# Inverse levels and tokens of a state-space layer done per whole block, at places beside the chain's stages of the same array tile

## The chip, the cores and the metric

The kernel runs on one core of one Trainium2 chip. The metric is the device time of one execution in microseconds (us), median of 3 runs.

## What is computed

A backbone of two layers over 512 latent and 256 context tokens of width 1024. In each layer a combined projection feeds two mixers side by side, a depthwise convolution of 31 taps with group norm, and a bidirectional RWKV-7 recurrence over 8 heads of 64; an output projection, and a SwiGLU feed-forward follow, all with modulation from the condition vectors. The recurrence is, per head and direction:

```python
def step(s, inp):
    r_t, k_t, v_t, w_t, kk_t, b_t = inp
    sa = -jnp.einsum("bhvk,bhk->bhv", s, kk_t)
    s = (s * w_t[:, :, None, :] + sa[..., None] * b_t[:, :, None, :]
         + v_t[..., None] * k_t[:, :, None, :])
    y = jnp.einsum("bhvk,bhk->bhv", s, r_t) if emit else None
    return s, y
```

It runs forward and backward over the context, and from the two final states over the latents. `y_f + y_b`, normalised per head, gated and joined with the convolution, goes through `w_out`.

## The kernel before

**Tiling.** The recurrence is done in chunks of 64 tokens. Two heads (a pair, 128 partitions) and both directions go together, so a layer has 4 pairs. The 12 chunks of a pair are 3 blocks of 4 chunks (`s` = 0 to 3), so a layer has 12 blocks `b` = 0 to 11. A block holds 8 (chunk, direction) places `q` for each of the two heads `hh`; a half `hf` is two of the four chunks.

**Steps of a block.** They are Python generators; each `yield` ends one step.
- `prep(b)`, 3 steps: decay, keys and so on into `KR` and `bk` (ScalarE, VectorE).
- `z_part(b)`, 3 steps: `grams` multiplies `bk` with `KR` on TensorE and masks the products on VectorE into `G`, one half a step; then `base(b)` inverts the 16x16 diagonal blocks of the chunk matrices. It writes `G` to DRAM (`d`), reads the diagonals back as `Dt`, runs 15 rounds of two VectorE operations on `xtmp` and `XT`, each dependent on the one before, copies `XT` once on ScalarE, and writes the result into an image in DRAM (`dimg`).
- `t_part(b, hf)`, 4 steps: `inverses` reads the image into `Tm` by DMA; `levels` grows the inverse from 16 to 64 with small products (`Tm`,`G` and `Tm`,`W` in tiles of 64x64, then 32x32) and copies between them; the last step puts `KR` into `G` for the chain.
- `tokens(b, hf)`, 2 steps: transposes of `bk` into `tT` and of the values into `UV`.
- `chain(b, s)`, 3 steps for each of four chunks: the serial part, from state `S` to the next: products `UV`,`G` (tile 128x64), copy to `Z`, `Z`,`Tm` (64x64), copy to `UV`, `UV`,`tT` (128x64), new `S`.

**Order.** TensorE's order is the program's order (`manual_schedule`); the other engines' orders are made by a scheduler from it. `weave` makes the program's order: each lane is `(first, slots, n, generator)`, its `n` steps stand at `first + slots*(i+1)/n` of a block of 16 slots, and all lanes of a block are sorted by that place. The lanes of block `b` hold the projection of later columns (`proj`), the modulation (`ada`), `chains(b)` at slots 1.33, 2.67, ... 16, convolution taps on VectorE, and the preparation of later blocks: `z_part(b + 2)`, `prep(b + 2)`, `t_part(b + 1, 0)`, and `t_part(b, 1)`. The places are in `PLAN`, one entry a layer; `prologue` holds those ahead of block 0, in units of a projection of 768 columns.

**Buffers.** `pd`, `pw`, `pc` are PSUM pools of 3, 3 and 2 banks; the levels and the tokens use `pw`, the chain `pc`. `Tm`, `tT` and `UV` have 4 buffers of half a block each. Every small operation is recorded under the line of a helper (`mm` 234, `act` 222, `tt` 228, `stt` 225), so that the trace is read by tile names.

Of the kernel before, what the change touches and what calls it, by code (L numbers as in the profile page):

```python
# [20 lines left out]
T = SX + SC  # L21
# [59 lines left out]
def _pack(i):  # L81
# [45 lines left out]
    for nf in FPARTS:  # L127
# [22 lines left out]
         lanes={"chains": (0, 16), "t1": (0, 4), "t0": (12, 4), "tok1": (0.6, 3.26), "tok0": (13, 2), "prep": (2, 4),  # L150
                "z": (9, 4), "bonus": (3.89, 12.11), "pair_prep": (8, 8), "pair_out": (0, 13)},
         prologue={"pair_prep": (-1.3, 1.2), "prep0": (-0.3, 0.8), "z0": (0.9, 0.58), "tok00": (1.99, 1.08), "tok01": (1.94, 0.38), "prep1": (2.4, 1.0),
                "z1": (3.58, 0.6), "t0": (3.89, 0.86), "tok10": (4.12, 0.2)},
# [4 lines left out]
         lanes={"chains": (0, 16), "t1": (0, 4), "t0": (12.5, 3.5), "tok1": (0, 2.35), "tok0": (13, 2), "prep": (2, 4),  # L158
                "z": (9, 5.03), "bonus": (1.41, 13.65), "pair_prep": (7.33, 7.84), "pair_out": (0, 13)},
         prologue={"pair_prep": (-1.7, 1.2), "prep0": (-0.44, 0.74), "z0": (0.93, 0.52), "tok00": (1.52, 0.47), "tok01": (1.79, 0.39), "prep1": (1.97, 0.98),  # L160
                "z1": (3.6, 0.6), "t0": (3.98, 0.73), "tok10": (4.3, 0.3)},
# [9 lines left out]
def net(ctx: ExitStack, tc: tile.TileContext, I, out):  # L171
# [369 lines left out]
    for l in range(DEPTH):  # L541
# [213 lines left out]
        def prep(b):  # L755
# [42 lines left out]
            BS[b] = dict(KR=KR, bk=bk, vr=vr, pc=pc, emit=emit, G={}, tT={}, UV={}, T={})  # L798
# [35 lines left out]
        def tokens(b, hf):  # L834

            p, gi = divmod(b, 3)
            P, B = PS[p], BS[b]
            bk = B["bk"]
            tT = s2.tile([128, 2, 4, 64], F32, tag="tT", name=nm("tT"), bufs=4)
            UV = s2.tile([128, 4, 2, 64], F32, tag="UV", name=nm("UV"), bufs=4)  # L840
            B["tT"][hf] = tT
            B["UV"][hf] = UV
            pt = [bank(), bank()]
            for s in range(2):
                for d in range(2):
                    cc = 2 * hf + s
                    o = 64 * (2 * s + d)
                    for hh in range(2):
                        hs = slice(64 * hh, 64 * hh + 64)
                        PE.transpose(pt[hh][:, o:o + 64],  # L850
                                     bk[hs, d, cc, hh:hh + 2, :].rearrange("p j t -> p (j t)"), ident[hs, hs])
            for hh in range(2):
                act(tT[:, hh, :, :], pt[hh][:, 0:256].rearrange("p (q j) -> p q j", j=64))
            yield
            pv = bank()
            for s in range(2):
                for d in range(2):
                    cc = 2 * hf + s
                    c0 = C * nat(0, gi, cc)
                    src = B["vr"][:, cc, :] if d else u[f"v{p}"][:, c0:c0 + 64]  # L860
                    o = 128 * (2 * s + d)
                    PE.transpose(pv[0:64, o:o + 128], src, ident)  # L862
            for hh in range(2):
                act(UV[64 * hh:64 * hh + 64, :, hh, :],
                    pv[0:64].rearrange("p (q h j) -> p q h j", q=4, h=2)[:, :, hh, :])
            yield
# [29 lines left out]
        def inverses(b, hf):  # L896

            Tm = s2.tile([128, 4, 2, 64], F32, tag="Tm", name=nm("Tm"), bufs=4)
            for hh in range(2):
                w = 64 - 64 * hh  # L900
                nc.sync.dma_start(out=Tm[w:w + 64].rearrange("p q x c -> p q (x c)"),
                                  in_=dimg[b % 3][8 * hf + 4 * hh:8 * hf + 4 * hh + 4, 0:8192]
                                  .rearrange("q (r c) -> r q c", c=128))
            BS[b]["T"][hf] = Tm

        def levels(b, hf):

            B = BS[b]
            Gt, Tm = B["G"][hf], B["T"][hf]
            lm = lmask.rearrange("p (x t) -> p x t", x=2)  # L910
            pW = bank()
            for q in range(4):
                for hh in range(2):
                    w = slice(64 - 64 * hh, 128 - 64 * hh)
                    mm(pW[w, 64 * q:64 * q + 64], Gt[w, hh, q, 0:64], Tm[w, q, 0, :])
            W = s2.tile([128, 4, 64], F32, tag="W", name=nm("W"))
            act(W.rearrange("p q t -> p (q t)"), pW[:, 0:256])
            yield
            pX = bank()
            for q in range(4):  # L920
                for hh in range(2):
                    w = slice(64 - 64 * hh, 128 - 64 * hh)
                    mm(pX[w, 64 * q:64 * q + 64], W[w, q, :], Tm[w, q, 1, :])
            for q in range(4):
                for hh in range(2):
                    w = slice(64 - 64 * hh, 96 - 64 * hh)
                    mm(pX[w, 256 + 32 * q:288 + 32 * q], Tm[w, q, 1, 0:32], W[w, q, 0:32])
            for hh in range(2):
                w = slice(64 - 64 * hh, 96 - 64 * hh)
                V.copy_predicated(out=Tm[w, :, 0, 0:32], mask=lm[w, 0:1, 0:32].to_broadcast([32, 4, 32]),  # L930
                                  data=pX[w, 256:384].rearrange("p (q t) -> p q t", t=32))
            V.copy_predicated(out=Tm[:, :, 1, :], mask=lm[:, 1:2, :].to_broadcast([128, 4, 64]),
                              data=pX[:, 0:256].rearrange("p (q t) -> p q t", t=64))
            yield
            pW = bank()
            W = s2.tile([128, 4, 64], F32, tag="W", name=nm("W"))
            for q in range(4):
                for hh in range(2):
                    w = 64 - 64 * hh
                    mm(pW[w + 32:w + 64, 32 * q:32 * q + 32], Gt[w:w + 32, hh, q, 32:64], Tm[w:w + 32, q, 0, 0:32])  # L940
            for hh in range(2):
                w = slice(96 - 64 * hh, 128 - 64 * hh)
                act(W[w, :, 0:32], pW[w, 0:128].rearrange("p (q t) -> p q t", t=32))
            yield
            pX = bank()
            for q in range(4):
                for hh in range(2):
                    w = 64 - 64 * hh
                    mm(pX[w:w + 32, 32 * q:32 * q + 32], W[w + 32:w + 64, q, 0:32], Tm[w + 32:w + 64, q, 1, 32:64])
            for hh in range(2):  # L950
                w = slice(64 - 64 * hh, 96 - 64 * hh)
                act(Tm[w, :, 1, 32:64], pX[w, 0:128].rearrange("p (q t) -> p q t", t=32))

            for hh in range(2):
                act(Gt[64 - 64 * hh:128 - 64 * hh, hh, :, 0:64].rearrange("p (s d) t -> p d s t", d=2),
                    B["KR"][64 * hh:64 * hh + 64, :, 2 * hf:2 * hf + 2, 0, :])
            yield

        def chain(b, s):
# [3 lines left out]
            Gt, tT, UV, Tm = (B[k][s // 2] for k in ("G", "tT", "UV", "T"))  # L963
# [8 lines left out]
            for d, hh in DH:  # L972
# [3 lines left out]
                mm(pz[w, 64 * d:64 * d + 64], Gt[k, hh, q, 0:64], UV[k, q, hh, :])  # L976
# [15 lines left out]
            for d, hh in DH:  # L992
                w = slice(64 - 64 * hh, 128 - 64 * hh)
                mm(pu[w, 64 * d:64 * d + 64], Tm[w, 2 * s_ + d, 1, :], Z[w, 64 * d:64 * d + 64])
            pu3 = pu[:, 0:128].rearrange("p (d t) -> p d t", d=2)
            with soon():
                act(UV[64:128, 2 * s_:2 * s_ + 2, 0, :], pu3[64:128], AF.Copy, scale=-1.0)
                ts(UV[0:64, 2 * s_:2 * s_ + 2, 1, :], pu3[0:64], -1.0, 0.0)
            yield

            if not fin:
                pm = bank("c")
                for d, hh in DH:
                    hs = slice(64 * hh, 64 * hh + 64)
                    mm(pm[hs, 64 * d:64 * d + 64], tT[:, hh, 2 * s_ + d, :], UV[:, 2 * s_ + d, hh, :])
                Sn = s2.tile([128, 2, 64], F32, tag="S", name=nm("S"))
                with soon():
# [8 lines left out]
                    Un = BS[bn]["UV"][sn // 2]  # L1016
                    act(Un[64:128, 2 * (sn % 2):2 * (sn % 2) + 2, 0, :], Sn[0:64])
                    act(Un[0:64, 2 * (sn % 2):2 * (sn % 2) + 2, 1, :], Sn[64:128])
                P["S"] = Sn
            if emit:  # L1020
                for d, hh in DH:
                    hs = slice(64 * hh, 64 * hh + 64)
                    q = 2 * s_ + d
                    mm(py[hs, 64 * d:64 * d + 64], UV[:, q, hh, :], Gt[:, hh, q, 64:128], S is None and d == 0, d == 1)
# [137 lines left out]
        def t_part(b, hf):  # L1162
            inverses(b, hf)
            yield from levels(b, hf)

        def chains(b):
            for s in range(4):
# [4 lines left out]
        with tc.manual_schedule(engines={mybir.EngineType.PE}):  # L1172
            for name, ps in zip(FIRST, pf):
# [3 lines left out]
            start = {"pair_prep": (pair_prep(0), 3), "prep0": (prep(0), 3), "z0": (z_part(0), 3), "tok00": (tokens(0, 0), 2),  # L1177
                     "tok01": (tokens(0, 1), 2), "prep1": (prep(1), 3), "z1": (z_part(1), 3), "t0": (t_part(0, 0), 4),
                     "tok10": (tokens(1, 0), 2)}
# [6 lines left out]
            for b in range(12):  # L1186
# [9 lines left out]
                lane("t1", t_part(b, 1), 4)  # L1196
# [197 lines left out]
```

## Time and profile before

| | |
|---|---|
| median of 3 runs | 2247.91 us (2246.09 to 2260.29) |
| the profiled execution's own time | 2251.84 us |
| its span | 2250.0 us |
| TensorE busy | 2134.0 us (95%) |
| VectorE, ScalarE, GpSimd busy | 1333.6, 952.3, 193.0 us |
| mean granted clock | 0.975 |
| mixing stage of layer 0, of layer 1 | about 105 to 590 us, about 1345 to 1815 us |

The span is the time from the program's first instruction to its last, the execution's time the whole on the device. The granted clock is the share of full speed that TensorE's clock got. A busy TensorE is not one at its peak, since its instructions overlap.

### The profile page before, as it was taken

What the parts mean: (1) busy time and instruction counts of PE and PEld (TensorE: products, weight loads), DVE (VectorE), ACT (ScalarE), POOL (GpSimd) and SP (SyncE); (2) the same over time, 40 slices, a digit from 0 to 9 for tenths busy, and PEclk for the clock granted to TensorE, in tenths of its full rate; (3) what the DMA queues carried; (4) which work ended last, traced back from release to release, by engine and by line L of the source; (5) the groups of instructions that cost most, each with busy time, mean ns of one, the idle gap of its engine ahead of it and who ended that gap; (6) DMA issues with size and microseconds to landing.
All of it is one profiled execution on the core that took longest, in us unless ns stands there. A gap on an engine that the chain in (4) does not pass through costs nothing.

```text
span 2250.0 us, 46614 instructions
## 1 busy us (share of the span) xinstructions
PE 2134.0 (95%) x18800; PEld 1724.2 (77%) x18800; DVE 1333.6 (59%) x3249; ACT 952.3 (42%) x2260; POOL 193.0 (9%) x524
## 2 busy tenths in 40 slices
PE   6999999999999999999999999999999989999996
PEld 4777777777687888888888776767676678888885
DVE  5578887878648332332333766778777755343446
ACT  5455645555325211211212545566656534222223
POOL 0102121312010000000000000121212010000000
PEclk9999999999799999999999999899999999999999
DMA  8233422333554112111122413132424552223223
GB/s 289 65 100 90 108 77 68 84 98 107 146 176 150 57 52 71 61 61 66 51 72 86 139 49 94 37 84 66 114 52 116 169 204 75 95 90 106 86 98 118
DMA packets 196007, 220.72 MB, mean 98 GB/s; under 512 B 110352, under 2 KB 139792, under 8 KB 195792
## 3 DMA queue, kind: packets, MB, share of 16 engines
q1 hardware_dynamic: 194640, 215.65, 31.9%
q8 instruction: 148, 2.42, 0.4%
q10 hardware_dynamic: 1152, 2.10, 0.2%
q14 instruction: 67, 0.55, 0.1%
HBM read 192.49 MB, written 25.21 MB: 97 GB/s over the span
## 4 chain that ended last, share of the span: by engine, by line
PE 77%; ACT 8%; DVE 7%; DMA 3%; POOL 2%; issue 2%; SPq 0%; POOLq 0%; ACTq 0%; DVEq 0%
PE pd L234 38%; PE pw L234 33%; PE pc L234 5%; ACT tmp L222 2%; ACT UV L222 1%; DVE wl L228 1%; DMA raw<-in_wd 1%; DMA Dt<-d 1%; PE pw L862 1%; ACT wh L222 1%; DVE acc L225 1%; PE pw L850 1%; ACT Tm L222 0%; DVE xtmp L228 0%; POOL rq L385 0%
## 5 line engine op out<-in xcount | busy, mean ns | idle before, releaser
L234 PE MATMUL pd<-h,wh 128*128 128x512 f32 (+2 forms) x2496 | 686.5, 364 | 6.6 <-ACT h L222 4.5
L222 ACT ACTIVATE wh<-raw 128x1024 fp32r<-128x1024 f32 (+2 forms) x234 | 220.6, 944 | 714.1 <-PE pw L234 317.2
L234 PEld LDWEIGHTS pd<-h,wh 128*128 128x128 f32 (+1 forms) x2496 | 424.9, 190 | 80.0 <-ACT h L222 5.8
L234 PE MATMUL pd<-h,wl 128*128 128x512 f32 (+2 forms) x1248 | 426.6, 365 | 0.0
L228 DVE TENSOR_TENSOR wl<-raw,wh 128x1024 fp32r<-128x1024 f32 (+2 forms) x234 | 252.6, 1081 | 239.1 <-ACT wh L222 237.6
L234 PE MATMUL pw<-h,wh 128*128 128x512 f32 (+1 forms) x1264 | 316.4, 349 | 1.7 <-DVE x L225 1.7
L234 PEld LDWEIGHTS pd<-h,wl 128*128 128x128 f32 (+1 forms) x1248 | 223.8, 189 | 35.7 <-issue 1.6
L234 PEld LDWEIGHTS pw<-h,wh 128*128 128x128 f32 x1264 | 210.3, 189 | 37.3 <-DVE x L225 1.9
L225 DVE SCALAR_TENSOR_TENSOR acc<-z,cw,acc 128x497 f32<-128x497 f32 (+9 forms) x336 | 209.7, 644 | 2.1 <-ACT acc L222 1.4
L234 PE MATMUL pw<-h,wl 128*128 128x512 f32 (+1 forms) x632 | 193.4, 351 | 0.0
L234 PE MATMUL pd<-mid,wh 128*128 128x512 f32 (+1 forms) x568 | 136.6, 344 | 5.0 <-ACT wh L222 4.9
L228 DVE TENSOR_TENSOR ft<-ft,pw 128x512 f32<-128x512 f32 (+1 forms) x67 | 37.8, 590 | 171.2 <-PE pw L234 170.8
L234 PE MATMUL pw<-mid,wh 128*128 128x512 f32 (+1 forms) x568 | 136.5, 343 | 0.6 <-ACT wh L222 0.6
L234 PEld LDWEIGHTS pw<-h,wl 128*128 128x128 f32 x632 | 106.9, 189 | 15.3
L234 PEld LDWEIGHTS pd<-mid,wh 128*128 128x128 f32 x568 | 93.4, 189 | 20.6 <-ACT wh L222 6.5
L234 PEld LDWEIGHTS pw<-mid,wh 128*128 128x128 f32 x568 | 93.7, 189 | 14.4 <-ACT wh L222 0.8
L970 POOL TENSOR_TENSOR Q<-S,pc 128x128 f32<-128x128 f32 x80 | 44.7, 559 | 537.7 <-DVE S L225 183.5
L234 PE MATMUL pd<-mid,wl 128*128 128x512 f32 (+1 forms) x284 | 87.6, 347 | 2.3 <-DVE wl L228 2.3
L234 PE MATMUL pw<-mid,wl 128*128 128x512 f32 (+1 forms) x284 | 87.4, 346 | 0.6 <-DVE wl L228 0.6
L225 DVE SCALAR_TENSOR_TENSOR x<-pw,mod,x 128x512 f32<-128x512 f32 (+1 forms) x60 | 40.1, 672 | 80.4 <-PE pw L234 80.4
L228 DVE TENSOR_TENSOR xtmp<-XT,Dt 64x15 f32<-64x15 f32 (+4 forms) x360 | 75.3, 209 | 11.5 <-DMA Dt<-d 7.2
L774 POOL MEMSET tmp<- 128x4 f32 x48 | 5.2, 108 | 876.3 <-PE pw L234 632.3
(190 smaller groups left out, 3298.0 us busy)
## 6 DMA issues: line engine op xcount, KB each, us to landing
ada<-in_ada SPq DMA_DIRECT2D x96, 512.0 KB, 4.2
raw<-in_wgu SPq DMA_DIRECT2D x88, 512.0 KB, 3.4
raw<-in_win SPq DMA_DIRECT2D x42, 512.0 KB, 3.4
raw<-in_wd SPq DMA_DIRECT2D x48, 320.0 KB, 2.9
Tm<-dimg SPq DMA_DIRECT2D x96, 128.0 KB, 3.6
raw<-in_wd SPq DMA_DIRECT2D x32, 384.0 KB, 3.0
d<-G SPq DMA_DIRECT2D x96, 64.0 KB, 2.1
raw<-in_wo SPq DMA_DIRECT2D x16, 384.0 KB, 3.2
```

The source lines that it names most:

```text
L222: A.activation(out=out, in_=in_, func=func, **k)
L225: V.scalar_tensor_tensor(out=out, in0=in0, scalar=scalar, in1=in1, op0=op0, op1=op1, **k)
L228: V.tensor_tensor(out=out, in0=a, in1=b, op=op)
L234: PE.matmul(out=out, lhsT=lhsT, rhs=rhs, start=start, stop=stop)
L774: G.memset(lx[:, :, 0:1], 0.0)
L850: PE.transpose(pt[hh][:, o:o + 64], bk[hs, d, cc, hh:hh + 2, :].rearrange("p j t -> p (j t)"), ident[hs, hs])
L862: PE.transpose(pv[0:64, o:o + 128], src, ident)
L970: G.tensor_tensor(out=Q, in0=S, in1=pc[:, :, s:s + 1].to_broadcast([128, 2, 64]), op=MUL)
```

## The change

Levels and tokens of a block are done for both halves at once. `t_part(b + 1)` runs in block `b` at four places given one by one, and `tokens(b + 1)` at two; the lanes `t0`, `t1`, `tok0` and `tok1` are gone. `Tm`, `tT` and `UV` have 2 buffers of a whole block. The number of matmuls and their shapes stay; the copies between the levels are one for both halves, the tT copies likewise. The second step of the levels takes two PSUM banks in place of one.

```diff
-         lanes={"chains": (0, 16), "t1": (0, 4), "t0": (12, 4), "tok1": (0.6, 3.26), "tok0": (13, 2), "prep": (2, 4),
+         lanes={"chains": (0, 16), "t": (0, (6.6667, 10.6667, 12.0000, 14.0000)), "tok": (0, (0.6, 1.3333)), "prep": (2, 4),
                 "z": (9, 4), "bonus": (3.89, 12.11), "pair_prep": (8, 8), "pair_out": (0, 13)},
-         lanes={"chains": (0, 16), "t1": (0, 4), "t0": (12.5, 3.5), "tok1": (0, 2.35), "tok0": (13, 2), "prep": (2, 4),
+         lanes={"chains": (0, 16), "t": (0, (6.6667, 10.6667, 12.0000, 14.0000)), "tok": (0, (0.6, 1.3333)), "prep": (2, 4),
                 "z": (9, 5.03), "bonus": (1.41, 13.65), "pair_prep": (7.33, 7.84), "pair_out": (0, 13)},
...
-        def inverses(b, hf):
-            Tm = s2.tile([128, 4, 2, 64], F32, tag="Tm", name=nm("Tm"), bufs=4)
-            for hh in range(2):
-                w = 64 - 64 * hh
-                nc.sync.dma_start(out=Tm[w:w + 64].rearrange("p q x c -> p q (x c)"),
+        def inverses(b):
+            Tm = s2.tile([128, 8, 2, 64], F32, tag="Tm", name=nm("Tm"), bufs=2)
+            for hf in range(2):
+                for hh in range(2):
+                    w = 64 - 64 * hh
+                    nc.sync.dma_start(out=Tm[w:w + 64, 4 * hf:4 * hf + 4].rearrange("p q x c -> p q (x c)"),
...
             pW = bank()
-            for q in range(4):
+            for q in range(8):
                 for hh in range(2):
                     w = slice(64 - 64 * hh, 128 - 64 * hh)
-                    mm(pW[w, 64 * q:64 * q + 64], Gt[w, hh, q, 0:64], Tm[w, q, 0, :])
-            W = s2.tile([128, 4, 64], F32, tag="W", name=nm("W"))
-            act(W.rearrange("p q t -> p (q t)"), pW[:, 0:256])
+                    mm(pW[w, 64 * q:64 * q + 64], G8(q)[w, hh, 0:64], Tm[w, q, 0, :])
+            W = s2.tile([128, 8, 64], F32, tag="W", name=nm("W"), bufs=1)
+            act(W.rearrange("p q t -> p (q t)"), pW)
             yield
-            pX = bank()
-            for q in range(4):
+            pX, pY = bank(), bank()
+            for q in range(8):
...
         def weave(*lanes):
-            order = sorted((first + slots * (warp((i + 1) / n) if warp else (i + 1) / n), j)
-                           for j, (first, slots, n, _, *w) in enumerate(lanes) for warp in [w[0] if w else None] for i in range(n))
-            for _, j in order:
+            order = []
+            for j, (first, slots, n, _, *w) in enumerate(lanes):
+                warp = w[0] if w else lambda q: q
+                at = slots if isinstance(slots, tuple) else [first + slots * warp((i + 1) / n) for i in range(n)]
+                order += [(at[i], j) for i in range(n)]
+            for _, j in sorted(order):
                 next(lanes[j][3], None)
...
                 lane("chains", chains(b), 12)
-                lane("t1", t_part(b, 1), 4)
...
                 if b + 1 < 12:
-                    lane("tok1", tokens(b + 1, 1), 2)
-                    lane("t0", t_part(b + 1, 0), 4)
+                    lane("tok", tokens(b + 1), 2)
+                    lane("t", t_part(b + 1), 4)
...
                     lane("z", z_part(b + 2), 3)
-                    lane("tok0", tokens(b + 2, 0), 2)
```

In the prologue `t0` now does all of block 0, at the same place, and `tok0` both halves; `tok01` and `tok10` are gone.

Where the levels of block 2 of the first layer begin on TensorE, before. `pd` rows are the projection, `Tm_437` is the first half's `Tm`, `Z`, `S`, `UV` and `pc` belong to the chain:

```order
L234 MATMUL pd_415_2482<-h_45_208,wh_334_1955 128x512
L234 MATMUL pw_438_2595<-Tm_437_2592,G_317_1867 64x64 x8
L234 MATMUL pc_445_2652<-UV_276_1629,G_230_1349 64x64 x4
L234 MATMUL pd_415_2482<-h_44_207,wl_335_1957 128x512
L234 MATMUL pd_415_2482<-h_46_209,wh_334_1955 128x512
L234 MATMUL pd_415_2482<-h_47_210,wh_334_1955 128x512
L234 MATMUL pd_415_2482<-h_46_209,wl_335_1957 128x512
L234 MATMUL pd_447_2665<-ada_425_2517,cs_133 32x128 x8
L234 MATMUL pw_450_2678<-Tm_437_2592,W_439_2604 64x64 x8
```

And after, for the same block (`Tm_388`, and `G_306` and `G_315` for its two halves):

```order
L234 MATMUL pd_325_2006<-h_45_208,wh_254_1599 128x256
L234 MATMUL pc_386_2392<-KR_205_1190,S_375_2314 64x64 x4
L234 MATMUL pc_387_2397<-Z_381_2363,Tm_293_1776 64x64 x4
L234 MATMUL pw_389_2409<-Tm_388_2404,G_306_1865 64x64 x8
L234 MATMUL pw_389_2409<-Tm_388_2404,G_315_1941 64x64 x8
L234 MATMUL pd_325_2006<-h_44_207,wl_255_1601 128x256
```

The 64x64 products of both halves now stand directly behind the chain's 64x64 products, of the second chunk of the block before. The last product of `KR` and `bk` for this block stands 161 rows further up in the order before, 104 rows further up in the order after.

VectorE at the end of `base` for that same block, before; `XT` and `xtmp` are `base`'s, `S` and `mod` the chain's and the modulation's, `acc` a convolution tap, `KR` and `tmp` the next `prep`:

```order
L228 TENSOR_TENSOR XT_340_1978<-XT_340_1978,xtmp_341_1979 64x12x4
L225 SCALAR_TENSOR_TENSOR S_398_2347<-pc_397_2342,pc_212_1205,Q_374_2216 128x64
L228 TENSOR_TENSOR xtmp_341_1979<-XT_340_1978,Dt_339_1977 64x39
L225 SCALAR_TENSOR_TENSOR S_398_2347<-pc_397_2342,pc_212_1205,Q_374_2216 128x64
L228 TENSOR_TENSOR XT_340_1978<-XT_340_1978,xtmp_341_1979 64x13x3
L779 SCALAR_TENSOR_TENSOR tmp_393_2314<-one65_95,tmp_393_2314 128x260
L228 TENSOR_TENSOR xtmp_341_1979<-XT_340_1978,Dt_339_1977 64x28
L231 TENSOR_SCALAR mod_265_1588<-pw_396_2339,prm_88 128x2
L228 TENSOR_TENSOR XT_340_1978<-XT_340_1978,xtmp_341_1979 64x14x2
```

And after:

```order
L228 TENSOR_TENSOR XT_330_2019<-XT_330_2019,xtmp_331_2020 64x12x4
L231 TENSOR_SCALAR mod_260_1628<-pw_373_2306,prm_88 128x2
L228 TENSOR_TENSOR xtmp_331_2020<-XT_330_2019,Dt_329_2018 64x39
L225 SCALAR_TENSOR_TENSOR acc_272_1661<-z_229_1363,cw_19_152,acc_272_1661 128x249
L228 TENSOR_TENSOR XT_330_2019<-XT_330_2019,xtmp_331_2020 64x13x3
L228 TENSOR_TENSOR KR_367_2282<-kk_312_1892,tmp_371_2288 128x4x64
L228 TENSOR_TENSOR xtmp_331_2020<-XT_330_2019,Dt_329_2018 64x28
L228 TENSOR_TENSOR KR_367_2282<-r_179_995,tmp_371_2288 128x4x64
L228 TENSOR_TENSOR XT_330_2019<-XT_330_2019,xtmp_331_2020 64x14x2
```

One foreign instruction stands between each two of `base`'s steps in both orders; what it is has changed, that it is there has not.

More of the change, by code (lines that the diff above doesn't have):

```diff
@@ L832, in grams, with tokens @@
                 yield
-        def tokens(b, hf):
+        def tokens(b):
             p, gi = divmod(b, 3)
-            P, B = PS[p], BS[b]
+            B = BS[b]
             bk = B["bk"]
[L839 to L842, printed above, removed]
+            tT = s2.tile([128, 2, 8, 64], F32, tag="tT", name=nm("tT"), bufs=2)
+            UV = s2.tile([128, 8, 2, 64], F32, tag="UV", name=nm("UV"), bufs=2)
+            B["tT"], B["UV"] = tT, UV
             pt = [bank(), bank()]
-            for s in range(2):
+            for cc in range(4):
                 for d in range(2):
-                    cc = 2 * hf + s
-                    o = 64 * (2 * s + d)
+                    o = 64 * (2 * cc + d)
                     for hh in range(2):
@@ L852, in tokens @@
             for hh in range(2):
-                act(tT[:, hh, :, :], pt[hh][:, 0:256].rearrange("p (q j) -> p q j", j=64))
+                act(tT[:, hh, :, :], pt[hh].rearrange("p (q j) -> p q j", j=64))
             yield
[L855 to L862, printed above, removed]
-            for hh in range(2):
-                act(UV[64 * hh:64 * hh + 64, :, hh, :],
-                    pv[0:64].rearrange("p (q h j) -> p q h j", q=4, h=2)[:, :, hh, :])
+            for hf in range(2):
+                pv = bank()
+                for s in range(2):
+                    for d in range(2):
+                        cc = 2 * hf + s
+                        c0 = C * nat(0, gi, cc)
+                        src = B["vr"][:, cc, :] if d else u[f"v{p}"][:, c0:c0 + 64]
+                        o = 128 * (2 * s + d)
+                        PE.transpose(pv[0:64, o:o + 128], src, ident)
+                for hh in range(2):
+                    act(UV[64 * hh:64 * hh + 64, 4 * hf:4 * hf + 4, hh, :],
+                        pv[0:64].rearrange("p (q h j) -> p q h j", q=4, h=2)[:, :, hh, :])
             yield
@@ L951, in levels @@
                 w = slice(64 - 64 * hh, 96 - 64 * hh)
[L952 to L956, printed above, removed]
+                act(Tm[w, :, 1, 32:64], pX[w, 0:256].rearrange("p (q t) -> p q t", t=32))
+            for hf in range(2):
+                for hh in range(2):
+                    act(B["G"][hf][64 - 64 * hh:128 - 64 * hh, hh, :, 0:64].rearrange("p (s d) t -> p d s t", d=2),
+                        B["KR"][64 * hh:64 * hh + 64, :, 2 * hf:2 * hf + 2, 0, :])
             yield
@@ L962, in chain @@
             KR, pc, emit = B["KR"], B["pc"], B["emit"]
-            Gt, tT, UV, Tm = (B[k][s // 2] for k in ("G", "tT", "UV", "T"))
+            Gt, tT, UV, Tm = B["G"][s // 2], B["tT"], B["UV"], B["T"]
             s_ = s % 2
@@ L1023, in chain @@
                     q = 2 * s_ + d
[L1024 removed]
+                    mm(py[hs, 64 * d:64 * d + 64], UV[:, 2 * s + d, hh, :], Gt[:, hh, q, 64:128], S is None and d == 0, d == 1)
                 for d in range(2):
@@ L1160, in z_part, with t_part @@
             yield
-        def t_part(b, hf):
-            inverses(b, hf)
-            yield from levels(b, hf)
+        def t_part(b):
+            inverses(b)
+            yield from levels(b)
         def chains(b):
```

66 lines of the change are left out of this document (33 added, 33 removed).

## Prediction

> **What bounds the kernel now.** I read the page first, then busy time by stage, then single instructions in order of time.
>
> ```profile
> PE 2134.0 (95%) x18800; PEld 1724.2 (77%) x18800; DVE 1333.6 (59%) x3249; ACT 952.3 (42%) x2260; POOL 193.0 (9%) x524
> 105.00:590.00 485.00, 455.85 (x5847) 355.51 (x5846) 397.55 (x1169) 272.88 (x777) 89.89 (x208) 0.95 0.36 95
> 1345.00:1815.00 470.00, 446.06 (x5572) 326.82 (x5571) 341.61 (x1014) 281.92 (x809) 76.37 (x226) 0.97 0.34 91
> ```
>
> The last two rows are the mixing stages of the two layers, where everything that the diff touches runs; their columns after the length are TensorE, its weight loads, VectorE, ScalarE and GpSimd busy, then granted clock and DMA. TensorE is busy 94% and 95% there, and idle 29 + 24 = 53 us. ScalarE is idle 44% and 40%. So the stages go at TensorE's pace, and TensorE runs a woven order written by hand: whatever stands first in it and waits, holds everything behind it. Two things then matter: what the order costs in issue, and what it would wait for.
>
> **What a change of array tile costs.** TensorE's instructions, in order of time: start, length, tile, form, count.
>
> ```profile
> 181.14 0.45 PE L234 MATMUL pc<-UV,tT 128*64 128x64 f32 x8
> 181.42 0.40 PE L234 MATMUL pc<-G,UV 128*64 128x64 f32 x8
> 185.75 0.68 PE L234 MATMUL pw<-Tm,G 64*64 64x64 f32 x16
> 186.36 0.45 PE L234 MATMUL pc<-UV,G 128*64 128x64 f32 x8
> 186.74 0.50 PE L234 MATMUL pd<-h,wl 128*128 128x512 f32 x1
> 187.07 0.63 PE L234 MATMUL pd<-h,wh 128*128 128x512 f32 x2
> 187.54 0.39 PE L234 MATMUL pd<-h,wl 128*128 128x512 f32 x1
> 187.86 0.64 PE L234 MATMUL pd<-ada,cs 128*32 128x128 f32 x16
> ```
>
> Starts count here, since lengths overlap. In the stream of 128x512 products, 187.07 to 187.54 is 0.235 us each. The first after a small tile takes 186.74 to 187.07 = 0.33, and the last ahead of one 187.54 to 187.86 = 0.32: about 0.10 to enter and 0.09 to leave. Eight records of tile 128*64 between two changes take 186.36 to 186.74 = 0.38; a like group with a change only ahead of it takes 181.14 to 181.42 = 0.28. So leaving a small tile is 0.10 too, and entering one I put at 0.05. A change into 128*128 costs 0.20 us, one into a smaller tile 0.15 us.
>
> **The change, part by part.**
>
> *Fewer changes of tile.* Counted over TensorE's whole order as built, neighbours differ in tile 1154 times before and 904 times after: 250 fewer, 35 of them into 128*128 and 215 into smaller tiles. 35 x 0.20 + 215 x 0.15 = **-39 us**, 1.6 us for each of 24 blocks. The number of matmuls is the same.
>
> *Fewer, wider copies.*
>
> ```profile
> L222 ACT ACTIVATE W<-pw 32x128 f32<-32x128 f32 x96 | 25.8, 269 | 1.8
> L222 ACT ACTIVATE W<-pw 128x256 f32<-128x256 f32 x48 | 18.1, 378 | 31.8 <-PE pw L234 26.8 <-PE pc L234 4.4
> L222 ACT ACTIVATE gy<-pw 128x512 f32<-128x512 f32 x16 | 9.4, 588 | 7.4 <-PE pw L234 7.4
> ```
>
> Each block had two W copies of 0.378 us and eight small ones of 0.269 us in the levels (the second step's and the last step's), and four tT copies of the 0.378 kind. Now there is one W and two tT of the 128x512 kind (0.588) and four small ones, somewhere between 0.269 and 0.378. ScalarE gains 4.4 - 3.0 = 1.4 us a block. I cost it at nothing: ScalarE is idle 40% or more of these stages. VectorE's masked copies go from six to three, each wider; also nothing. The levels' second step and the tokens now ask for more PSUM banks of the pool of three at once: between 0 and one 0.588 us evacuation twice in each of 24 blocks, 0 to 28 us. I take 0, because the new wait below lets those copies run empty.
>
> *The earlier place of the levels.* This is the term that decides. The levels' first product needs `Tm`, which comes out of a long chain: second `grams` product, mask on VectorE, DMA to `d`, DMA to `Dt`, 30 dependent VectorE steps, one ScalarE copy, DMA to `dimg`, DMA to `Tm`. Block b=2 of the first layer shows it (the SPq lines are DMA issues, with the time the queue was at them):
>
> ```profile
> 167.73 1.16 PE L234 MATMUL pw<-KR,bk 64*128 64x128 f32 x16
> 173.66 0.59 SPq L881 DMA_DIRECT2D Dt<-d  x1
> 178.89 0.15 DVE L228 TENSOR_TENSOR xtmp<-XT,Dt 64x15 f32<-64x15 f32 x1
> 197.43 0.17 DVE L228 TENSOR_TENSOR XT<-XT,xtmp 64x15 f32<-64x15 f32 x1
> 160.00:207.00 47.00, 6.90 (x30) 0.64 (x1) 0.42 (x2) 1.00 0.33 88
> 202.70 2.57 SPq L901 DMA_DIRECT2D Tm<-dimg  x4
> DMA to landing us min/median/max: 2.5/3.6/5.2
> 212.42 0.68 PE L234 MATMUL pw<-Tm,G 64*64 64x64 f32 x16
> ```
>
> The products end at 168.89. `Dt` is asked for 4.8 us later, the 30 steps run from 178.89 to 197.60, and the first two of four `Tm` DMAs land about 202.70 + 0.6 + 3.6 = 206.9 (the issues stand 0.6 apart; the landing row is that of line 901). That is a **chain of 38 us**, and `Tm` is used at 212.42: 5.5 us to spare. The 30 steps hold only 6.9 us of work (first number of the windows row, which counts instructions on `XT`), yet take 18.7, since VectorE's queue has another instruction between each two. A block whose queue is nearly free of those runs shorter, as b=9 of the second layer:
>
> ```profile
> 1669.30 1.11 PE L234 MATMUL pw<-KR,bk 64*128 64x64 f32 x16
> 1691.99 2.57 SPq L901 DMA_DIRECT2D Tm<-dimg  x4
> 1707.21 0.68 PE L234 MATMUL pw<-Tm,G 64*64 64x64 f32 x16
> ```
>
> 1670.41 to 1691.99 + 0.6 + 3.6 = 1696.2, a chain of 26 us. Now the distance that covers the chain. A block is 16 slots:
>
> ```profile
> 129.51 1.16 PE L234 MATMUL pw<-KR,bk 64*128 64x128 f32 x16
> 543.38 1.56 PE L234 MATMUL pw<-KR,bk 64*128 64x128 f32 x16
> 1363.46 1.16 PE L234 MATMUL pw<-KR,bk 64*128 64x128 f32 x16
> 1739.79 1.16 PE L234 MATMUL pw<-KR,bk 64*128 64x128 f32 x16
> ```
>
> These are the second grams products of b=1 and b=11 in each layer. 414.3/10 = 41.4 us a block in the first, 376.3/10 = 37.6 in the second. In the first layer those products stand at slot 9 + 4 x 2/3 = 11.67, and the levels of the same block began at slot 13 of the next: 17.3 slots x 2.59 = 44.9 us (43.5 measured above). Now they begin at slot 6.67 of the next: 11.0 slots x (41.4 - 1.6)/16 = **27.4 us**. In the second layer 10.3 slots x (37.6 - 1.6)/16 = **23.2 us**. The chain of 38 doesn't fit, that of 26 hardly.
>
> Does the chain get shorter? Its VectorE part can be read off the built queue. Of the 12 blocks of the first layer, seven (b = 2, 4, 5, 7, 8, 10, 11) still have 28 or 29 foreign instructions among the 30 steps, the count of b=2 before; in the second layer four have 27 or 28 (b = 2, 5, 7, 11). The rest have 1 to 12. I take 38 us for the long ones and 27 for the others, between the 26 of the short row and a little for the middling ones. The first block of each layer keeps its place in the prologue.
>
> First layer: 7 x (38 - 27.4) = 74. Second: 4 x (38 - 23.2) + 7 x (27 - 23.2) = 59 + 27 = 86. **+160 us** of waiting on TensorE, ahead of the first `Tm`,`G` product. Behind it stands the whole woven order: the projection, the state chain, the next grams, so that the next block's chain starts later by as much and nothing catches up.
>
> *What is given back.* While TensorE stands, ScalarE, VectorE and GpSimd empty their queues, and waits that it had on them shrink. There are 53 us of idle time to regain; between 0 and 53, I take three quarters, **-40**, as the new wait comes in nearly every block.
>
> *The clock.*
>
> ```profile
> 1303.01:1307.04 4.03, 0.01 (x1) 0.00 (x0) 3.27 (x7) 3.51 (x6) 0.46 (x3) 1.00 0.61 195
> 1307.23:1314.06 6.83, 6.83 (x23) 5.86 (x23) 2.98 (x5) 0.91 (x2) 3.15 (x14) 0.50 0.00 0
> ```
>
> TensorE idle for 4.03 us was followed by 6.83 us at a granted clock of 0.50, which can lose 3.4 us. For the 11 long waits: 0 to 37, and since what follows the levels is mostly streamed projection I take **+37**. The Trainium skill, "TensorE: Matmul & The Clock Gate", section "Why this matters for your kernels", asks for no idle gaps above about 3 us between bursts, because one idle window brings the slow clock back. It speaks against this change. The slow stretch here was two of the 3.4 us windows that the page gives; with one, this term would be an estimated 19 and the sum 18 us lower.
>
> **Sum.** -39 + 160 - 40 + 37 = +118 us on the profiled execution, 2251.84 us (span 2250.0): 2370. The median shown is 2247.91, 4 us less, so I predict **2366 us**.
>
> **Rivals.**
>
> *The chain is covered after all.* If the base chain stays below 27.4 us in the first layer and 23.2 in the second (say, because VectorE, freed of waiting for TensorE, rushes through the foreign instructions), only the -39 is left: 2209 us. Against it: 6.9 us of steps and four DMAs in a row take 26 us even in the short row, and the foreign instructions are work, not waits. 0.07.
>
> *All chains short.* If all 22 run as the short row, 27 us, the second layer alone waits: 11 x 3.8 = 42. With -39 and some idle time regained, -10 to 0, the time is within 1%: about 2241 to 2251. For it: VectorE gets idle time in a longer block. Against: the count of foreign instructions is fixed in its queue. 0.06.
>
> *It doesn't do what it says.* If the drain at a change of tile was hidden in the waits, the -39 shrinks to about a quarter, -10, with the rest as forecast: about 2395. For it: some changes of tile do stand at waits. Against: the 0.32 and 0.33 stand in an unbroken stream. Inside my range; 0.12.
>
> *The forecast*, 0.75.
>
> **How the numbers follow.** Low end of the forecast: chains 2 us shorter in 18 blocks (-36), all 53 regained (-13), no clock loss (-37): 2280. High end: nothing regained (+40), banks (+28), and the levels held for the last of the four DMAs, 1.2 us later, in 18 blocks (+22): 2456. Not all of these come together, so the range is 2285 to 2440. It leaves out the two rivals below and little of the rest. 1% is about what a measurement of this kernel can tell from no change; faster by more 0.07, within 0.06, slower 0.87.
>
> **What would show it.** In the profile after: TensorE's longest waits in both mixing stages ahead of `Tm`,`G` products, named for the `Tm` DMA or for what comes ahead of it, 5 to 15 us in the blocks with a full VectorE queue and little in the others; blocks of 44 to 50 us in place of 41.4 and 37.6; TensorE busy well under 90% there; granted clock below 0.95. The feed-forward stages (590 to 1345 and 1815 on) must not change in length. Wrong would be the chain's length if `Tm` lands within 30 us of the grams in the blocks named, the distance if the levels' place is reached later than 28 us, and the tile term if starts of neighbours are as now.

## The result and the profile after

2431.51 us (median of 4 runs, 2426.61 to 2440.43), against 2251.06 for the kernel before beside it: a ratio of 1.081, 95% interval 1.078 to 1.084. The change makes the kernel slower. The profiled execution took 2426.61 us, its span is 2424.7 us, its mean granted clock 0.937. Against the span of before that is +174.7 us; the prediction's sum was +118. One execution of all those told of below, of the kernel with `z` at 6.5, took 2994.80 us at a granted clock of 0.64 and is left out of that kernel's time.

The engines' row of the page, the clock's row of its slices, the chain that ended last, and a window in each of the two mixing stages, which now end at about 706 and 1987 us (length, then TensorE, its weight loads, VectorE, ScalarE, GpSimd busy, clock, DMA):

```profile
PE 2154.4 (89%) x18800; PEld 1747.0 (72%) x18800; DVE 1330.9 (55%) x3177; ACT 933.1 (38%) x2092; POOL 192.1 (8%) x524
PEclk9999899988699999999999998988899799999999
PE pd L234 36%; PE pw L234 31%; PE pc L234 5%; DMA Tm<-dimg 3%; DMA dimg<-XT 2%; DVE acc L225 1%; SPq L901 1%; DVE xtmp L228 1%; DMA Dt<-d 1%; DVE XT L228 1%; DVE wl L228 1%; ACT wh L222 1%; ACT UV L222 1%; PE pw L861 1%; DMA raw<-in_wd 1%
```

```profile
105.00:655.00 550.00, 462.78 (x5862) 366.40 (x5861) 408.41 (x1157) 265.08 (x701) 87.93 (x208) 0.89 0.32 85
1400.00:1930.00 530.00, 413.61 (x5035) 306.98 (x5033) 325.79 (x941) 255.81 (x680) 70.76 (x207) 0.88 0.26 69
```

TensorE is busy 84% and 78% of these windows, where it was 94% and 95%; the clock fell from 0.95 and 0.97 to 0.89 and 0.88. Over the whole span TensorE's idle time grew by 154.3 us (2250.0 - 2134.0 = 116.0 to 2424.7 - 2154.4 = 270.3), its busy time by 20.4. The chain that ended last now runs through the parts of `base`: `Dt`, `xtmp` and `XT`, `dimg`, `Tm`. What TensorE waited for (us in total, times, longest):

```profile
PE pw L234 <- DMA Tm<-dimg: 156.8, 46, 15.0
PE pc L234 <- DVE acc L228: 17.3, 2, 15.8
...
PE pw L861 <- ACT tT L222: 5.4, 8, 1.0
PE pw L234 <- DVE Tm L929: 5.4, 12, 0.9
```

The first row alone is the 154. The second, nearly all of it ahead of the program's first products, is as before. The last two, on the merged copies, are new (the kernel before had 0.3 on its masked copies). The block that the prediction followed, b=2 of the first layer, in order of time (start, length; the SPq rows are DMA issues, the queue's time at them):

```profile
169.02 1.17 PE L234 MATMUL pw<-KR,bk 64*128 64x128 f32 x16
174.90 0.59 SPq L880 DMA_DIRECT2D Dt<-d  x1
180.16 0.16 DVE L228 TENSOR_TENSOR xtmp<-XT,Dt 64x15 f32<-64x15 f32 x1
197.14 0.17 DVE L228 TENSOR_TENSOR XT<-XT,xtmp 64x15 f32<-64x15 f32 x1
201.63 2.57 SPq L901 DMA_DIRECT2D Tm<-dimg  x4
204.18 0.47 PE L234 MATMUL pw<-Tm,G 64*64 64x64 f32 x2 [6.06 <-DMA Tm<-dimg]
205.06 2.35 PE L234 MATMUL pw<-Tm,G 64*64 64x64 f32 x30 [0.41 <-DMA Tm<-dimg]
```

The grams products end at 170.19. TensorE was ready for the levels at 204.18 - 6.06 = 198.12, 27.9 us later (predicted cover: 27.4). The first `Tm` halves were there after 34.0 us, not 38: the 30 steps took 17.2 us instead of 18.7, and what stands around them, mostly the way from the last step to the landing, about 2.5 less; the landing in the 38 was itself an estimate. The products of the second half of `Tm` then waited 0.41 more, for the last two of the four DMAs.

The second grams products of b=1 and b=11 of each layer give the blocks' length:

```profile
127.32 1.16 PE L234 MATMUL pw<-KR,bk 64*128 64x128 f32 x16
600.54 1.16 PE L234 MATMUL pw<-KR,bk 64*128 64x128 f32 x16
1426.23 1.16 PE L234 MATMUL pw<-KR,bk 64*128 64x128 f32 x16
1896.06 1.16 PE L234 MATMUL pw<-KR,bk 64*128 64x128 f32 x16
```

47.3 us a block in the first layer and 47.0 in the second, where there were 41.4 and 37.6. What lies outside the two stretches from the first grams product to the last `Z`,`Tm` product took 1221.2 us, before 1224.6: the feed-forward stages did not change.

### The profile page after: what moved, and what is told of

It is laid out like the page before. It is cut to its first block, busy times and chain, and to the rows that moved or that the text cites. A ratio compares the mean times of both kernels' runs of the same rounds, so it can differ in the third digit from the quotient of the medians.

```text
span 2424.7 us, 46238 instructions
## 1 busy us (share of the span) xinstructions
PE 2154.4 (89%) x18800; PEld 1747.0 (72%) x18800; DVE 1330.9 (55%) x3177; ACT 933.1 (38%) x2092; POOL 192.1 (8%) x524
## 4 chain that ended last, share of the span: by engine, by line
PE 73%; DVE 9%; DMA 8%; ACT 5%; issue 2%; POOL 2%; SPq 1%; POOLq 0%; DVEq 0%; ACTq 0%
PE pd L234 36%; PE pw L234 31%; PE pc L234 5%; DMA Tm<-dimg 3%; DMA dimg<-XT 2%; DVE acc L225 1%; SPq L901 1%; DVE xtmp L228 1%; DMA Dt<-d 1%; DVE XT L228 1%; DVE wl L228 1%; ACT wh L222 1%; ACT UV L222 1%; PE pw L861 1%; DMA raw<-in_wd 1%
## 5 line engine op out<-in xcount | busy, mean ns | idle before, releaser
L234 PE MATMUL pd<-h,wh 128*128 128x512 f32 (+2 forms) x2496 | 694.1, 368 | 7.0 <-ACT h L222 4.5
L234 PEld LDWEIGHTS pd<-h,wh 128*128 128x128 f32 (+1 forms) x2496 | 430.7, 193 | 81.1 <-ACT h L222 5.4
L234 PE MATMUL pw<-Tm,G 64*64 64x64 f32 (+1 forms) x1536 | 75.6, 249 | 160.7 <-DMA Tm<-dimg 156.8
L234 PEld LDWEIGHTS pw<-Tm,G 64*64 64x64 f32 (+1 forms) x1536 | 62.0, 156 | 173.3 <-DMA Tm<-dimg 133.2
L972 POOL TENSOR_TENSOR Q<-S,pc 128x128 f32<-128x128 f32 x80 | 54.1, 676 | 624.0 <-DVE S L225 336.4
```

What stands on the lines that cost most here:

```text
L234: PE.matmul(out=out, lhsT=lhsT, rhs=rhs, start=start, stop=stop)
L972: G.tensor_tensor(out=Q, in0=S, in1=pc[:, :, s:s + 1].to_broadcast([128, 2, 64]), op=MUL)
```

## Experiments

Two theories stood against each other. *Place*: the levels stand too near to the grams, and TensorE waits for `base`; merging the halves costs nothing in itself. *Merging*: doing both halves at once is what costs (wider copies, four DMAs, more banks). Prices of the sum, the tile change and the clock, were tested apart. Times without a ratio are single runs; ratios are to the kernel before, with their 95% interval.

**The place alone.** The kernel before, halves apart as they were, with only the lane of the first half moved, so that its first step stands where the change has it (the other three come earlier than there):

```diff
-         "t0": (12, 4)          # layer 0;  (12.5, 3.5) in layer 1
+         "t0": (5.3333, 5.3333) # both layers
```

> The kernel before, halves still apart, with one thing changed: the first half's levels (t0) begin at slot 6.67 of the block ahead (steps at 6.67, 8, 9.33, 10.67) in place of 13. 1132 changes of tile, near the 1154 of before. Theory: the first Tm,G product waits as in the change: 130 to 160 us on the Tm DMA, 2400 to 2470 us. Rival (merging): no merging here, so 2250 us, give or take 1%.

2406.28 us, span 2404.5. Its engines, and what TensorE waited for most:

```profile
PE 2158.3 (90%) x18800; PEld 1749.3 (73%) x18800; DVE 1339.9 (56%) x3249; ACT 958.2 (40%) x2260; POOL 192.3 (8%) x524
...
PE pw L234 <- DMA Tm<-dimg: 147.9, 38, 16.5
```

Most of the loss, 154.5 of the 174.7 us in the spans, with no merging: 148 us of the same wait, though TensorE's order has only 22 changes of tile fewer than before. The time and the wait came as the theory said. The idle time beside this wait is 2404.5 - 2158.3 - 147.9 = 98.3 us, where the kernel before has 116.0 in all.

**The merging alone.** The change with its levels where the first half's stood before:

```diff
-         "t": (0, (6.6667, 10.6667, 12.0000, 14.0000))
+         "t": (0, (13.0, 14.0, 15.0, 16.0))
```

> The merging without the early place: both halves at once, the four steps of the levels at 13, 14, 15 and 16 in both layers, about where the first half's lane stood before. By place the cover is within 2 us of the kernel before, so no Tm wait; z, prep and tokens as in the change. TensorE's order has 192 changes of array tile fewer than before. Theory with the price that the two kernels with extra products give (38 us for 589 changes, 0.065 us each): about 12 us less than before, 2230 to 2250 us. With the price of the prediction's sum (39 us for 250): 30 us less, 2215 to 2225. Rival (doing both halves at once has a price of its own, as the 15 to 18 us over the kernel before suggest that the two best placed merged kernels kept): 2255 to 2270, without Tm or bk waits.

2253.75 us (2243.78 to 2266.62), a ratio of 1.002, interval 1.000 to 1.005: no difference that matters. Its engines and longest waits, among them those that the kernel before hardly had:

```profile
PE 2126.6 (94%) x18800; PEld 1722.0 (76%) x18800; DVE 1332.6 (59%) x3177; ACT 928.9 (41%) x2092; POOL 200.5 (9%) x524
...
PE pw L861 <- ACT Tm L222: 10.2, 9, 1.7
PE pw L234 <- DVE Tm L933: 9.8, 18, 1.6
...
PE pw L234 <- DMA Tm<-dimg: 4.4, 4, 2.4
```

With the place undone, 157 us of `Tm` wait become 4.4. TensorE is busy 7.4 us less than before, for 192 changes of tile fewer; its idle time is 16.5 us more (2259.1 - 2126.6 = 132.5; this execution was 7 us slower than the median). The levels' own copies now show as waits: the masked copy of `Tm` 9.8, and the tokens' bank held by ScalarE's copy of `Tm` 10.2 (a like row had 4.4 before). So 7.4 of the theory's 12 us were there as busy time, and more than that was spent as waits: merging has a price of its own, about as large as its gain. The 39 us of the sum did not show. The time lies between the two expectations, 4 us above the theory's and 1 below the rival's, whose cause, a price of the merging itself, is the one that the waits show.

**The levels later, two ways.** First with the chain's places kept, then evenly spread:

```diff
-         "t": (0, (6.6667, 10.6667, 12.0000, 14.0000))
+         "t": (0, (10.6667, 14.6667, 15.4, 16.5))   # first kernel
+         "t": (0, (10.6667, 12.6, 14.3, 16.0))      # second kernel
```

> The change with the levels four slots later: places 10.67, 14.67, 15.4 and 16.5 in place of 6.67, 10.67, 12 and 14. The first step stays beside the chain's 64x64 products, the built order has 901 changes of tile (904 in the change). Theory (the base chain, 26 to 38 us, is longer than its cover): the cover grows by four slots, to about 36 us in layer 0 and 31 in layer 1, so only the long chains of layer 1 still wait: 20 to 60 us of waits on the Tm DMA in place of 157, less time at the slow clock, about 2240 to 2310 us. Rival (the merging itself costs: wider bursts, two PSUM banks at once, whole-block buffers): the merging is all still there, so 2400 us or more.

> The change with its four steps of the levels at places 10.6667, 12.6, 14.3 and 16.0 in both layers, z and prep as in the change. By place on TensorE the distance from the second grams product to the levels is about 9 us longer than in the change, and grams stand no earlier, so prep's bk is ready for them. Theory (the wait is the distance against base's chain, and nothing in the merging itself costs time): the Tm wait falls from 157 to 10 to 35 us in the long blocks of both layers, waits on masked copies of Tm stay below 15, no wait on bk; 2250 to 2285 us. Rival (doing both halves at once has a price of its own, whatever the place): Tm and bk waits are small and the time is still 2290 or more, with the rest in waits on the levels' own copies or on ScalarE.

The first took 2303.39 us, ratio 1.025 (1.021 to 1.029), the second 2266.35, ratio 1.007 (1.005 to 1.009). Waits of the first:

```profile
PE pw L234 <- DVE Tm L933: 36.1, 38, 2.9
...
PE pw L234 <- DMA Tm<-dimg: 17.1, 11, 5.8
```

And of the second:

```profile
PE pw L234 <- DMA Tm<-dimg: 15.3, 13, 3.8
```

Four slots, some 9 us of cover, take the `Tm` wait from 157 to 15 to 17 us, and what is left stands mostly in the second layer's long chains. In the first kernel the third step came 0.73 slots behind the second, too close for the masked copy: 36 us in a new place, which the spread removes. Both times came as expected; the first kernel's `Tm` wait came a little below its 20 to 60 us.

**Grams earlier.** The spread levels, with `z` moved to slot 7, or with `z` at 6.5 and the levels from 9.33:

```diff
-         "z": (9, 4)                                                # 5.03 in layer 1
+         "t": (0, (10.6667, 12.6, 14.3, 16.0)),         "z": (7, 4)   # first
+         "t": (0, (9.33334, 10.66667, 13.33334, 16.0001)), "z": (6.5, 4) # second
```

> The merged levels at places 10.67, 12.6, 14.3 and 16, and the grams and base two slots earlier (z at 7 with 4 slots in both layers), so that the cover of the chain is about 17 slots again, as before the change (about 40 and 37 us), and the steps stand 1.7 to 1.9 slots apart. 938 changes of tile, 216 fewer than before. Theory (cover and spacing set the waits, fewer changes of tile gain): under 15 us of waits on the Tm DMA, under 10 on the masked copies; between 0 and 30 us faster than before, 2220 to 2255 us. Rival (merging costs by itself, by banks and bursts): 2270 us or more although the Tm DMA is not waited for.

> As the run before, with the levels' steps directly behind stages of the chain (9.33, 10.67, 13.33, 16) and z at 6.5: 918 changes of tile, cover 16.5 slots. Theory: the same waits, 20 changes of tile fewer are 3 us, so 2215 to 2255 us. Rival (merging costs by itself): 2270 us or more.

2297.11 us, ratio 1.021 (1.014 to 1.028), and 2349.15, ratio 1.043 (1.036 to 1.049). Both theories failed. The rival's 2270 or more came, but not for its reason: the longest wait by far is one that neither foresaw. Longest waits of the first, then of the second:

```profile
PE pw L234 <- DVE bk L225: 53.3, 22, 4.6
```

```profile
PE pw L234 <- DVE bk L225: 80.3, 23, 5.3
```

The `Tm` wait is all but gone in both (0.6 and 4.0 us); grams now reach TensorE ahead of `prep`'s `bk`. One wait took the other's place, from the far end of the same chain.

**prep earlier too.** The first of these with the two steps of `prep` that make `bk` earlier, and with `z` at 7 and at 8:

```diff
-         "prep": (2, 4)                    # 3.33, 4.67, 6
+         "prep": (0, (1.9, 2.9, 6.0)), "z": (7, 4)   # first
+         "prep": (0, (1.9, 2.9, 6.0)), "z": (8, 4)   # second
```

> As the kernel with the levels spread and z from slot 7 (2297 us, 53 us of waits on bk), but the first two steps of prep, which make bk, moved 1.4 and 1.8 slots ahead (places 1.9 and 2.9 for 3.33 and 4.67). Theory (that kernel's remaining loss is grams standing ahead of bk): waits on bk fall from 53 to below 20 us, Tm waits stay below 10; 2235 to 2270 us. Rival (VectorE and GpSimd are late with bk because of what stands ahead of it in their queues, not because of its place): waits on bk stay at 35 us or more and the time stays within 15 us of 2297.

> The same with z from slot 8 in place of 7: half of the advance of grams. By place the cover is 37 and 33 us, 2 us less than with slot 7. Theory: waits on bk below 10 us, Tm waits 5 to 15; 2225 to 2260 us, the fastest of the merged kernels and about as fast as the kernel before (2251). Rival as for slot 7: waits on bk 20 us or more, 2275 or more.

2293.09 us, ratio 1.018 (1.016 to 1.021), and 2269.18, ratio 1.008 (1.007 to 1.010).

```profile
PE pw L234 <- DVE bk L225: 26.2, 15, 4.7
```

```profile
PE pc L234 <- ACT UV L222: 22.3, 25, 3.0
...
PE pw L234 <- DVE XT L228: 8.0, 4, 3.9
...
PE pw L234 <- DVE bk L225: 3.8, 6, 1.2
```

With `z` at 7 the wait on `bk` was halved, between the two theories, and the time stayed; what took it back is not settled. In the profiled execution, the slowest of its four at a clock of 0.952, TensorE was busy 33 us longer (2162.5 against 2129.3) and worked 209 us at half clock in place of 160; why is open. With `z` at 8 `Tm` and `bk` are hardly waited for (3.3 and 3.8 us), yet the time is 9 us over what was expected: the chain's copy into `UV` on ScalarE is now late by 22 us in place of 8.2.

**A shorter chain.** The change with `base`'s 30 steps on GpSimd, so that no VectorE work stands between them:

```diff
-                tt(tv, X[...], Dt[...], MUL)
-                tt(X[...], X[...], tv, ADD)
+                G.tensor_tensor(out=tv, in0=X[...], in1=Dt[...], op=MUL)
+                G.tensor_tensor(out=X[...], in0=X[...], in1=tv, op=ADD)
```

> The change with the 30 steps of base on GpSimd in place of VectorE; the cover is the change's. GpSimd's queue has few other instructions, its small ones take 0.21 to 0.24 us in the trace (rq), so the steps should take 7 to 12 us in every block in place of 10 to 20. Theory (the foreign instructions in VectorE's queue make the chain long): chains of 26 to 30 us, waits of 30 to 80 us in place of 157, 2290 to 2350 us. Rival (the DMAs and landings make it long, or GpSimd is far slower at these shapes): waits as in the change or longer, 2420 us or more.

2439.76 us, span 2438.0: the expectation failed; the time is the rival's, the waits are not. Waits of TensorE, then one of ScalarE:

```profile
PE pw L861 <- ACT tT L222: 53.8, 13, 10.5
PE pc L234 <- ACT UV L222: 43.5, 22, 7.9
...
PE pw L234 <- DMA Tm<-dimg: 11.3, 9, 3.7
```

```profile
ACT XT L222 <- POOL XT L889: 193.1, 24, 14.6
```

The wait on `Tm` fell to 11 us, but that doesn't show that a shorter chain removes it. Here are the grams of block b=2 of the first layer and the levels' first product:

```profile
184.74 1.18 PE L234 MATMUL pw<-KR,bk 64*128 64x128 f32 x16
...
226.57 1.10 PE L234 MATMUL pw<-Tm,G 64*64 64x64 f32 x32
```

TensorE comes to the levels 40.7 us behind the grams and doesn't wait; in the change it was there after 27.9. The first `Tm` DMA lands 34.7 us behind the grams, in the change 33.9. Over blocks 1 to 11 of the two layers the chain from the grams to this landing is on average 29.6 and 26.9 us long, in the change 31.6 and 29.0: 2 us less. TensorE is ready after 35.2 and 28.7 us, in the change after 26.6 and 21.3. With this chain and the change's TensorE, some 105 of the 141 us of these first waits would have remained. So the wait went because TensorE came later; whether a chain short enough would remove it was not tested.

Why TensorE came later is seen in order of time: the first and last of the 30 steps on GpSimd, the copy on ScalarE that waits for them, and what stands behind it:

```profile
1748.90 0.70 POOL L888 TENSOR_TENSOR xtmp<-XT,Dt 64x15 f32<-64x15 f32 x1 [15.58 <-DMA Dt<-d]
...
1761.76 0.22 POOL L889 TENSOR_TENSOR XT<-XT,xtmp 64x15 f32<-64x15 f32 x1
...
1762.01 0.63 ACT L222 ACTIVATE XT<-XT 64x256 f32<-64x256 f32 x1 [10.06 <-POOL XT L889]
1762.67 0.64 ACT L222 ACTIVATE UV<-S 64x128 f32<-64x128 f32 x2
...
1763.03 1.02 PE L234 MATMUL pc<-UV,G 128*64 128x64 f32 x8 [7.90 <-ACT UV L222]
```

ScalarE stands 10.06 us at the copy of `XT`, and the state chain's copy into `UV`, for which TensorE waits 7.90 us, comes directly behind it. ScalarE stood so 24 times, 193.1 us in all, in the change 5 times and 10.8 us. TensorE's waits of over 2 us on the copies into `tT`, `UV`, `Z` and `Tm` are 143 us, and 114 of them fall into times when ScalarE stands there. The chain's `Q` = `S` times decay, on GpSimd behind the loop, is late too: 17 of the 80 begin over 2 us behind their `S`, in the change one.

**The clock.** The change with 178 products of 128x128x384 (356 records) ahead of the levels' first product in the blocks that wait, their result overwritten, so that TensorE stays busy in the wait:

```diff
             pW = bank()
+            for _ in range(KEEP[l][b]):
+                mm(pW[:, 0:384], ident, cst[:, 0:384])
```

> The change with 178 extra matmuls, 128x128 by 384 columns of fp32, about 0.65 us each, right ahead of the levels' first product, in each block about 85% of the wait that the change shows there (3 to 19 of them, none in blocks 0 and 1). Their result is overwritten; nothing is left out. They also add 40 changes of tile (6 us). Theory (part of the loss is the slow clock that follows the waits): the waits are filled, TensorE keeps its clock, and the kernel gets faster although it does 116 us more work: 30 to 55 us below the change, 2375 to 2400. Rival (the clock costs nothing, only the waits do): 2430 us or more.

2418.77 us, span 2417.0, TensorE busy 2264.7 (110 more), granted clock 0.963.

```profile
PE pw L235 <- DMA Tm<-dimg: 43.0, 54, 2.8
```

The wait fell by 114 us, the busy time rose by 110, and the time fell by 8 in the spans, so neither expectation came. By the trace's record of the clock TensorE's own work at half clock fell from 196 us to 159 (99 in the kernel before), and the added products were at half clock for 6 of their 123 us. The 37 us can have cost 18 at most; the 123 us that stand where 114 us of waiting were take 9 of that back. An estimate of 9 us agrees with the 8. But the change's own executions lie 14 us apart, and this is a single one: that the slow clock costs something is likely, not shown.

**The price of a tile change.** The kernel before with small products added in the streams of `dense`, outside the mixing stages; once as 32x32 products, once the same 32 columns in the full tile. The results are not used:

```diff
+            if k in (1, 3):
+                mm(bank("c")[0:32, 0:32], ident[0:32, 0:32], ident[0:32, 0:32])   # first
+                mm(bank("c")[:, 0:32], ident, ident[:, 0:32])                     # second
```

> The kernel before, with two extra 32x32 products of 32 columns in each step-group of the plain matrix products (`dense`: feed-forward and output projection), where TensorE runs without waits; result unread, nothing is left out. 597 more changes of tile than before, 291 of them into 128x128. Theory (0.20 us into 128x128, 0.15 into a small tile): 104 us for the changes and under 10 for the products, 2350 to 2370 us. Rival (the drain costs nothing, only the product does): 2255 to 2265 us.

> The control of the run before: the same extra products in the full tile of 128x128, 8 more changes of tile than before. Each is an fp32 product of few columns, 0.11 us a record and two records in the trace (`cst` against `ev`), 0.22 us with 292 of them: 64 us, so 2300 to 2320 us if that price holds, and in no case as slow as the run with small tiles.

2363.08 and 2335.70 us. The first came as expected, for a reason that the second takes away: that one, 16 us over its own expectation, has 8 changes of tile more than before and still cost 71 us outside the mixing stages (1295.3 against 1224.6). 1333.4 - 1295.3 = 38 us remain for 589 changes, **0.065 us each**. One place in each, TensorE in order of time, the small tile first:

```profile
833.76 0.88 PE L234 MATMUL pd<-mid,wh 128*128 128x512 f32 x4
834.47 0.51 PE L234 MATMUL pd<-mid,wl 128*128 128x512 f32 x2
834.91 0.24 PE L234 MATMUL pc<-cst 32*32 32x32 f32 x2
835.09 0.98 PE L234 MATMUL pd<-mid,wh 128*128 128x512 f32 x4
835.90 0.51 PE L234 MATMUL pd<-mid,wl 128*128 128x512 f32 x2
836.25 0.51 PE L234 MATMUL pd<-mid,wh 128*128 128x512 f32 x2
```

```profile
836.81 0.51 PE L234 MATMUL pd<-mid,wl 128*128 128x512 f32 x2
837.16 0.30 PE L234 MATMUL pc<-cst 128*128 128x32 f32 x2
837.30 0.96 PE L234 MATMUL pd<-mid,wh 128*128 128x512 f32 x4
838.10 0.51 PE L234 MATMUL pd<-mid,wl 128*128 128x512 f32 x2
```

From `wl` to the next `wl` it is 1.43 us with the small tile and 1.29 with the full one; undisturbed it is 0.71 (833.76 to 834.47) + 0.35 (835.90 to 836.25) = 1.06. Two changes of tile cost 0.14 us, 0.07 each. The short product costs 0.23 without them; some of that is the four wide products behind it, which take 0.80 to 0.81 instead of 0.71 in both kernels alike. At 138 such places in each kernel, at full clock and without waits, the starts on both sides of a short product lie 0.50 us apart with the small tile and 0.37 with the full one (medians): 0.06 for each change.

## Why the prediction was right or wrong

The sign, the cause and the range (2285 to 2440) held; the time was 65 us too low. The distances and the chance of slower held too: of what was to show it, the waits named for the `Tm` DMA, the blocks of 44 to 50 us (47.3 and 47.0), a busy share well under 90%, a clock below 0.95 and the unchanged feed-forward stages are all there; only the other blocks of the second layer, from which little was expected, wait up to 7.2 us. Term by term:

- *Waiting for `Tm`*, +160: 156.8 measured. The mechanism is right; that the total is so close is in part luck, since the pieces are less exact. In the first layer the waits ahead of the first product are 57 us for 74: 49 in the seven blocks named (6.1 to 8.0 each for 10.6) and 8 in three others. The first `Tm` DMA lands 30 to 42 us behind the grams in the blocks named and 22 to 26 in the others, and the distance to TensorE varies too, from 21 to 36 us. In the second layer they are 86 for 86: the four blocks named for 14.8 each wait 13.4, 10.1, 14.6 and 15.0, and the other seven 33 for 27. The short second waits for the last two DMAs make up the rest.
- *Given back*, -40: **over-estimated**, and what it was set against was left out. Idle time other than the `Tm` wait is 270.3 - 156.8 = 113.5 us, against 116.0 in all before: -3. Two effects meet there. With the place alone it is 98.3 us, so emptied queues do give back 18: the waits on `bk` and on ScalarE's copy into `UV` fall from 5.1 and 8.2 us to 0.3 and 3.9. With the merging alone it is 132.5 - 4.4 = 128.1, so the merging, with its wider copies and more banks at once, costs 12, where the prediction took 0 because the new wait would let those copies run empty. Together that is -6.
- *Fewer changes of tile*, -39: **over-priced**. At 0.065 us, 250 changes are 16. What went wrong is the reading of 0.32 and 0.33 us against 0.235 as the change's price: the control has the same lengthened step behind a short product without any change of tile.
- *The clock*, +37: of that size, but not settled more closely. TensorE's busy time rose by 20.4; with 16 less for the tiles, 36 are left for work done at half clock. With the place alone, where 22 changes of tile went, the same reckoning gives 24.3 + 1.4 = 26. By the record of the clock TensorE worked 196 us at half clock, before 99; the 97 us more can have cost 48 at most.

The span's sum was 57 us too low: -3 in place of -40 and -16 in place of -39 make 60, and the wait and the clock, 3 and 1 below their terms, take 4 off (the 16 is the control's price, and the clock's 36 what it leaves). The rest of the 65 is how the median stands to the profiled execution, 4 us below it in the prediction and 4.9 above it after.

Of the rivals, the one in which the chain is covered was priced at 2209 us. The merging alone is that case, brought about by place, and it takes 2254: even there no gain was to be had.

No merged kernel beat the one before. The best stands at a ratio of 1.002, and the next two at 1.007 and 1.008.

## What to carry to other kernels

Before a consumer is moved forward in an order written by hand, measure the producer's chain from its first input to its landing, and the distance in the order, block by block: the shortfall comes back as waiting, and everything behind it moves along. Old idle time shrinks a little under a new wait (18 of 116 us here); set against it what the change itself adds in waits, measured without the new wait. A price read from the neighbourhood of an event needs a control that has the neighbourhood without the event. And a wait that goes away is a proof only if the engine that waited still comes as early as before.

## What the runs showed of the hardware

A change of array tile costs 0.06 to 0.07 us here, less than half of what the starts around it suggest; most of the lengthening beside a small product is there for a short product in the full tile as well (1.29 against 1.06 us). The Trainium skill, "TensorEngine Tiling (Array Packing)", section "Key Properties", says that a change of tiling mode drains TensorE; the two kernels show that a change costs time, and how much, not by what.

A wait of 6.06 us slowed what followed it, by the windows of the change's trace (length, TensorE, weight loads, VectorE, ScalarE, GpSimd, clock):

```profile
207.34:212.80 5.46, 5.46 (x32) 4.43 (x31) 4.01 (x9) 2.61 (x6) 0.40 (x1) 0.51 0.00 0
212.80:216.00 3.20, 3.20 (x47) 2.36 (x46) 0.00 (x0) 0.56 (x2) 0.00 (x0) 1.00 0.30 73
```

TensorE is at half clock for 5.5 us of unbroken work and more ahead of it, then at full clock. The rule on idle gaps that the prediction drew from the Trainium skill, "TensorE: Matmul & The Clock Gate", section "Why this matters for your kernels", agrees with this row and with the stages' 0.89 and 0.88.

GpSimd did the 30 dependent steps in 12.0 and 12.5 us (mean of blocks 1 to 11 of each layer) where VectorE took 14.4 and 13.7 with other work between them. ScalarE, whose next copy waits for the last of these steps, stood idle for 193.1 us at it in place of 10.8, and the copies behind it were late.
